# Walking the tokens of the weight-stream matmuls from last to first, with weight tiles at one address distance

## The chip, the core and the metric

The kernel runs on one core of a Trainium2 chip. TensorE (PE) multiplies, VectorE (DVE) and ScalarE (ACT) do elementwise work, GpSimd (POOL) a little of it, and SyncE (SP) issues most of the transfers. SBUF is the working memory of 128 partitions, PSUM the small memory into which TensorE writes. The metric is the time of one execution on the device in microseconds, as the median of several runs; lower is better.

## The reference

Two layers of a hybrid block run over 272 tokens (16 learned ones and 256 of the input) of width 1024. Each layer is a mixer with three branches (retention, a gated recurrence, differential attention) and a feed-forward part with a short convolution. Cut to the products with weights, which the change touches:

```python
def mixer(hn, w_in, w_branch, w_out, ...):
    proj = (hn @ w_in).astype(F32)
    ...
    y_b = jnp.einsum('blnc,ncd->blnd', branches, w_branch.astype(F32))
    gates = jax.nn.sigmoid(mg.reshape(b, l, N_BRANCH, D_MODEL))
    y = jnp.sum(gates * y_b, axis=2)
    return y.astype(hn.dtype) @ w_out

def conv_ffn(hn, w_ffn_in, conv_w, conv_b, w_ffn_out, valid):
    u = jnp.where(valid[None, :, None], hn @ w_ffn_in, 0.0)
    ...
    return (jax.nn.silu(gate) * val) @ w_ffn_out
```

All weights are float32 and are used once per execution.

## The kernel before

Activations lie with features on the partitions and tokens along the row, so a product with a 128 x 128 tile of weights is one matmul whose stationary operand is the weight tile and whose moving operand is a row of up to 272 tokens. The output, 128 output features by the tokens, adds up in a PSUM bank over the 8 (or 22) feature tiles k of the input.

Each float32 operand is split into a high part that TensorE takes exactly in its fast format and a low part that holds the rest. The product is then three passes (lines 915 to 917): high weights by high input, high weights by low input, low weights by high input. This text calls them the stream passes. In layer 0 (and for keys and values in layer 1) a pass has 272 columns, the long form. In layer 1 the others leave out the first 14 tokens (T0) and have 258 columns, the short form. The last product of layer 1 (`fo`, lines 1520 to 1522) is done the other way round, with the weights as moving operand of 512 columns, and isn't part of what the diff edits.

`_Weights.next` (from line 612) brings the weights in chunks of 8 tiles, one DMA of 512 KB each (two halves for the first two). ScalarE writes the high parts to `whi`, VectorE the low parts to `wlo`. Each of these has 4 buffers, the raw chunk 3. Where in its buffer each tile stands is worked out by `_places` (line 131): the start of a tile, modulo 256 bytes (`LINE`), is brought to a wanted value. That value follows the moving operand: rows of 272 words are 1088 bytes, 64 more than a multiple of 256, so it grows by 64 for each k, modulo 256. It has an offset `APART`, one for the long form and one for the short, and 64 more (`BLOCK`) for inputs that lie in other tiles (b0, b1, b2, y, and the gated product). `_runs` (line 156) turns the places into as few instruction patterns as it can.

The moving operands are the normed input (`xh`, `xl`, in pairs of 4 rows of 272 words), the branches' outputs (`b0hi`, `b0lo` and so on), their sum (`yhi`, `ylo`) and the gated product (`ghi`, `glo`). All outputs are the PSUM tile `main`, two banks, one per output tile of a pair.

The order of all instructions is written by a planner (`_Plan`) from modelled costs and due times; each engine then runs its list as it stands. A group of three passes is one operation of the planner. The function `run` inside `products` issues it:

Of the kernel before, what the change touches and what calls it, by code (L numbers as in the profile page):

```python
# [88 lines left out]
def _ktiles(name):  # L89
    return FK if name == "fo" else KD  # L90
# [30 lines left out]


LINE = 256
APART = (0, 200)
BLOCK = 64
ROOM = CHUNK_TILES * P + 2 * LINE // 4
T0 = META - 2
# [3 lines left out]
def _places(depth=DEPTH):  # L131
# [4 lines left out]
    for li in range(depth):  # L136
        for name, j, k, _ in sum(_turns(li), []):
# [3 lines left out]
            short = li == DEPTH - 1 and name not in FULL  # L141
            wants.append(APART[short] + BLOCK * (name[0] == "b" or name in ("wo", "fo")) + 64 * (k % 4))
    out = []
# [497 lines left out]
        return self.cut  # L641


def build(tc, a, depth=DEPTH, probe=None):
    with ExitStack() as ctx:
        plan = _Plan(tc)
        _trace(ctx, tc, plan, a, depth, probe or {})
        plan.issue()
    return plan


def _trace(ctx, tc, plan, a, depth, probe):
# [19 lines left out]
    def new(pool_, shape, dt, tag, bufs, name):  # L672
        serial[0] += 1
        return plan.tile(pool_, shape, dt, tag, bufs, f"{name}_{serial[0]}")
# [217 lines left out]
    def products(xs, name, j, t0=0):  # L892

        if name in BASE or name == "fi":
            norm.next()
        if ahead:
            return ahead.pop()
        tiles = turns.pop(0)
        main = lambda: new(mp, [P, 2, 512], F32, "main", 2, "main")[:, :, t0:T]
        ps = {i: main() for i in sorted({x[1] for x in tiles})}  # L900
        to = {x: ps[x[0]][:, x[1], :] for x in {x[1::2] for x in tiles}}
        if (name, j) == ("fo", 3):

            to[j, 1] = main()[:, 1, :]
        cost = 3 * ((T - t0) / 2400 + 0.003)
        left = dict.fromkeys(to, _ktiles(name))
        for _, i, k, f in tiles:
            hi, lo = (x[:, t0:] for x in xs(k))
            begun = left[i, f] < _ktiles(name)
            left[i, f] -= 1  # L910
            plan.key = clock[0]
            wh, wl = weights.next()

            def run(o=to[i, f], wh=wh, wl=wl, hi=hi, lo=lo, first=not begun, last=left[i, f] == 0):
                nc.tensor.matmul(o, wh, hi, start=first, stop=False)  # L915
                nc.tensor.matmul(o, wh, lo, start=False, stop=False)  # L916
                nc.tensor.matmul(o, wl, hi, start=False, stop=last)  # L917

            plan.main.append(plan.add("pe", run, cost, [to[i, f]], [wh, wl, hi, lo], count=6))
            clock[0] += cost  # L920
        plan.key = clock[0] - 1.0
        if (name, j) == ("fo", 3):
            return [to[j, f] for f in range(2)]
        ahead.extend(ps[i] for i in ps if i != j)
        return ps[j]
# [71 lines left out]
    for li in range(depth):  # L997
# [477 lines left out]
        def block(name):  # L1475
            if name not in st:
                st[name] = slot4(name)
            return st[name]
# [65 lines left out]
        for name, j in ORDER:  # L1544
# [18 lines left out]
            elif name[0] == "*":  # L1563
# [4 lines left out]
                else:  # L1568
                    t = st["rg" if n == "b0" else "hg"]
# [6 lines left out]
            if name in BASE:  # L1576
                lo = 0 if name in FULL else t0
# [17 lines left out]
                elif name in ("dq", "dk"):  # L1595
                    t = block(f"{name}{j // 2}")
# [27 lines left out]
                else:  # L1624
                    t = block(f"{name}{j // 2}")
# [21 lines left out]
            elif name == "wo":  # L1647
                hi, lo = st["yhi"], st["ylo"]
# [40 lines left out]
            else:  # L1689
                hi, lo = st["ghi"], st["glo"]  # L1690
# [35 lines left out]
```

## Time and profile before

| what | value |
|---|---|
| time, median of 3 runs (lowest to highest) | 1301.39 us (1300.91 to 1302.28) |
| span of the profiled execution | 1299.9 us |
| TensorE, matmuls | busy 1290.8 us, 10965 instructions |
| TensorE, loads of weights | busy 1268.7 us, 10965 instructions |
| VectorE | busy 993.4 us |
| ScalarE | busy 855.9 us |
| bytes moved by DMA | 219.01 MB, mean 168 GB/s |
| mean granted TensorE clock | 0.999 |

The span is the time from the first to the last instruction of the one execution that was profiled; the runs' times have a little around it. Busy time of TensorE counts a matmul from its start to the modelled end of its output. Matmuls overlap, so their durations add up to more than the span, and what a pass costs is read from the distance of the starts. In a group's row stand the busy time and the mean duration in ns, and behind the second bar the time that the engine was idle just ahead of these instructions and who ended it. In the rows of a tile stand the smallest, the median and the largest duration.

### The profile page before, as it was taken

To read this page: it belongs to the slowest core of one execution; us is meant where nothing else is said; L and a number is where in the kernel's file an instruction comes from. 1 tells how busy PE (TensorE), PEld (TensorE's weight loads), DVE (VectorE), ACT (ScalarE), POOL (GpSimd) and SP (SyncE) were. 2 spreads that over 40 slices of the span, in tenths; PEclk is the share of its full clock that TensorE was granted. 3 is DMA by queue.
4 is the path that set the end of the run, shared out by engine and by line. 5 is a ranking of instruction groups with operands and counts; after the bars stand their busy time and mean duration, and the time that the engine had idled before them with its cause. 6 is when DMAs were issued, how large, how long until landed. Compare 5 with 4: busy or idle time off the path is not lost.

```text
span 1299.9 us, 27225 instructions
## 1 busy us (share of the span) xinstructions
PE 1290.8 (99%) x10965; PEld 1268.7 (98%) x10965; DVE 993.4 (76%) x1745; ACT 855.9 (66%) x1490; POOL 85.6 (7%) x162
## 2 busy tenths in 40 slices
PE   9999999999999999999999999999999999999998
PEld 8999999999999999999999999999999999999986
DVE  7685888698686789886565868886997868899753
ACT  6765565766777568776456664657667876787743
POOL 5000000000100020000020000000001100200000
PEclk9999999999999999999999999999999999999999
DMA  8555444435544555555555455454444456556653
GB/s 279 195 159 155 167 149 154 146 136 158 162 143 152 180 161 184 187 173 170 178 179 181 161 171 171 146 172 140 149 161 163 146 163 197 173 186 202 201 183 109
DMA packets 60751, 219.01 MB, mean 168 GB/s; under 512 B 6864, under 2 KB 6992, under 8 KB 60624
## 3 DMA queue, kind: packets, MB, share of 16 engines
q1 hardware_dynamic: 60336, 216.74, 51.6%
q8 instruction: 86, 1.41, 0.4%
q10 hardware_dynamic: 288, 0.52, 0.1%
q14 instruction: 41, 0.34, 0.1%
HBM read 216.19 MB, written 1.05 MB: 167 GB/s over the span
## 4 chain that ended last, share of the span: by engine, by line
PE 95%; DVE 3%; DMA 1%; issue 0%; SPq 0%; POOL 0%; ACT 0%; DVEq 0%
PE main L917 28%; PE main L915 28%; PE main L916 27%; PE fo L1520 2%; PE fo L1522 2%; PE fo L1521 2%; PE ds L1383 1%; PE do L593 1%; PE ro L593 1%; PE ho L593 1%; DMA wraw<-in_w 1%; PE vt L593 1%; DVE wlo L593 1%; PE wt L593 0%; PE lev L1106 0%; PE ms L593 0%
## 5 line engine op out<-in xcount | busy, mean ns | idle before, releaser
L915 PE MATMUL main<-xh,whi 128*128 128x272 f32 (+1 forms) x2368 | 687.8, 290 | 0.7 <-ACT whi L593 0.7
L917 PE MATMUL main<-xh,wlo 128*128 128x272 f32 (+1 forms) x2368 | 679.5, 287 | 0.5 <-DVE wlo L593 0.4
L916 PE MATMUL main<-xl,whi 128*128 128x272 f32 (+1 forms) x2368 | 670.4, 283 | 0.0
L593 DVE TENSOR_TENSOR wlo<-wraw,whi 128x1024 fp32r<-128x1024 f32 (+1 forms) x408 | 496.0, 1222 | 198.7 <-ACT whi L593 195.4
L593 ACT ACTIVATE whi<-wraw 128x1024 fp32r<-128x1024 f32 (+1 forms) x408 | 426.5, 1048 | 214.0 <-PE main L916 137.5
L916 PEld LDWEIGHTS main<-xl,whi 128*128 128x128 f32 x2368 | 449.3, 190 | 0.2
L915 PEld LDWEIGHTS main<-xh,whi 128*128 128x128 f32 x2368 | 445.5, 188 | 2.1 <-ACT whi L593 0.9
L917 PEld LDWEIGHTS main<-xh,wlo 128*128 128x128 f32 x2368 | 444.6, 188 | 1.4 <-DVE wlo L593 1.4
L593 DVE SCALAR_TENSOR_TENSOR two_b<-u,small,two_b 128x256 f32<-128x256 f32 (+2 forms) x176 | 78.3, 485 | 0.7 <-ACT two_b L593 0.2
L593 POOL TENSOR_TENSOR y<-h,rstd 128x272 f32<-128x272 f32 x32 | 38.2, 1225 | 311.1 <-ACT rstd L593 311.1
L917 PE MATMUL main<-ghi,wlo 128*128 128x272 f32 x176 | 51.0, 290 | 0.0
L915 PE MATMUL main<-ghi,whi 128*128 128x272 f32 x176 | 50.8, 288 | 0.0
L916 PE MATMUL main<-glo,whi 128*128 128x272 f32 x176 | 50.2, 285 | 0.0
L593 ACT ACTIVATE two_b<-u,small 128x272 f32<-128x272 f32 (+1 forms) x88 | 49.3, 598 | 0.7 <-DVE glo L593 0.5
L593 ACT ACTIVATE u<-main 128x544 f32<-128x544 f32 (+1 forms) x40 | 24.5, 612 | 36.5 <-PE main L917 36.4
L915 PE MATMUL main<-b0hi,whi 128*128 128x272 f32 (+1 forms) x128 | 37.3, 292 | 0.0
L915 PE MATMUL main<-b1hi,whi 128*128 128x272 f32 (+1 forms) x128 | 37.3, 292 | 0.0
L917 PE MATMUL main<-yhi,wlo 128*128 128x272 f32 (+1 forms) x128 | 36.5, 286 | 0.0
L917 PE MATMUL main<-b2hi,wlo 128*128 128x272 f32 (+1 forms) x128 | 36.5, 285 | 0.0
L917 PE MATMUL main<-b0hi,wlo 128*128 128x272 f32 (+1 forms) x128 | 36.5, 285 | 0.0
L917 PE MATMUL main<-b1hi,wlo 128*128 128x272 f32 (+1 forms) x128 | 36.5, 285 | 0.0
L915 PE MATMUL main<-b2hi,whi 128*128 128x272 f32 (+1 forms) x128 | 36.4, 284 | 0.0
(268 smaller groups left out, 1951.7 us busy)
## 6 DMA issues: line engine op xcount, KB each, us to landing
wraw<-in_w SPq DMA_DIRECT2D x402, 512.0 KB, 3.6
h<-in_h SPq DMA_DIRECT2D x4, 272.0 KB, 5.3
dec<-in_dec SPq DMA_DIRECT2D x2, 544.0 KB, 4.5
wraw<-in_w SPq DMA_DIRECT2D x4, 256.0 KB, 5.0
const<-in_const SPq DMA_DIRECT2D x1, 937.0 KB, 6.8
gain<-in_gl SPq DMA_DIRECT2D x1, 512.0 KB, 5.1
out<-y ACTq DMA_DIRECT2D x2, 256.0 KB, 2.7
out<-y SPq DMA_DIRECT2D x2, 256.0 KB, 2.7
```

The costliest lines, as they stand in the source:

```text
L593: self.plan.add(self.name, lambda: f(*args, **kw), cost, outs, ins, args[2] if method == "activation" else None, count)
L915: nc.tensor.matmul(o, wh, hi, start=first, stop=False)
L916: nc.tensor.matmul(o, wh, lo, start=False, stop=False)
L917: nc.tensor.matmul(o, wl, hi, start=False, stop=last)
L1383: nc.tensor.matmul(ss[m][:, at : at + nk], q[half, hd, q0 : q0 + P], k[half, hd, :nk], start=True, stop=True)
L1520: nc.tensor.matmul(o, gh, wh, start=False, stop=False)
L1521: nc.tensor.matmul(o, gl, wh, start=False, stop=False)
L1522: nc.tensor.matmul(o, gh, wl, start=False, stop=end)
```

## The change

```diff
-APART = (0, 200)
+APART = (80, 80)

+def backwards(t):
+
+    return bass.AP(t.tensor, t.offset + t.shape[1] - 1, [list(t.ap[0]), [-1, t.shape[1]]])

             def run(o=to[i, f], wh=wh, wl=wl, hi=hi, lo=lo, first=not begun, last=left[i, f] == 0):
+                o, hi, lo = (backwards(x) for x in (o, hi, lo))
                 nc.tensor.matmul(o, wh, hi, start=first, stop=False)
                 nc.tensor.matmul(o, wh, lo, start=False, stop=False)
                 nc.tensor.matmul(o, wl, hi, start=False, stop=last)
```

`backwards` makes a view of the same words that starts at the last one and steps by -1. In each stream pass the moving operand and the output are walked that way, so token 271 is read first and its column is written first; every token still lands in its own column. The stationary operand, the weight tile, keeps its step of +1 and is contiguous. `APART` sets the weight tiles at another distance from the moving operands, 80 bytes for the long and the short form alike, where it was 0 and 200.

## Prediction

> **What bounds the kernel now.** I read the page's busy shares first, then its chain of waits, then the list of who waited for whom, and then the groups by shape.
>
> ```profile
> span 1299.9 us, 27225 instructions
> PE 1290.8 (99%) x10965; PEld 1268.7 (98%) x10965; DVE 993.4 (76%) x1745; ACT 855.9 (66%) x1490; POOL 85.6 (7%) x162
> PEclk9999999999999999999999999999999999999999
> PE 95%; DVE 3%; DMA 1%; issue 0%; SPq 0%; POOL 0%; ACT 0%; DVEq 0%
> PE warm L593 <- POOL ones_d L593: 1.0, 1, 1.0
> PE main L915 <- ACT whi L593: 0.7, 1, 0.7
> PE main L917 <- DVE wlo L593: 0.4, 2, 0.2
> PE wt L593 <- POOL dt L593: 0.4, 1, 0.4
> PE ro L593 <- DVE am L593: 0.4, 1, 0.4
> PE ro L593 <- DVE wts L593: 0.2, 1, 0.2
> ```
>
> TensorE carries 95% of the chain, at full granted clock, and the last six lines are every wait it had: 3.1 us in all. There is no idle time to win. Only the length of the passes can move the end, and nearly all of them stand on three lines:
>
> ```profile
> L915 PE MATMUL main<-xh,whi 128*128 128x272 f32 x1536 | 450.5, 293 | 0.7 <-ACT whi L593 0.7
> L916 PE MATMUL main<-xl,whi 128*128 128x272 f32 x1536 | 436.7, 284 | 0.0
> L915 PE MATMUL main<-xh,whi 128*128 128x258 f32 x832 | 237.3, 285 | 0.0
> L917 PE MATMUL main<-ghi,wlo 128*128 128x272 f32 x176 | 51.0, 290 | 0.0
> L917 PE MATMUL main<-yhi,wlo 128*128 128x272 f32 x64 | 18.6, 291 | 0.0
> L915 PE MATMUL main<-yhi,whi 128*128 128x258 f32 x64 | 17.9, 280 | 0.0
> ```
>
> Each of the three lines has 1536 long passes on the normed input, 176 on the gated product and 64 each on b0, b1, b2 and y: 1968, so 5904 long ones. Short ones: 832 + 4 x 64 = 1088 a line, 3264 in all. These 9168 are what the diff edits.
>
> A duration of 290 ns is not what a pass costs, because passes overlap. The timeline shows it, with the load of the next weights under each pass:
>
> ```profile
> 539.84 0.28 PE L916 MATMUL main<-xl,whi 128*128 128x272 f32 x1
> 539.85 0.19 PEld L917 LDWEIGHTS main<-xh,wlo 128*128 128x128 f32 x1
> 539.96 0.29 PE L917 MATMUL main<-xh,wlo 128*128 128x272 f32 x1
> 539.97 0.19 PEld L915 LDWEIGHTS main<-xh,whi 128*128 128x128 f32 x1
> 540.09 0.29 PE L915 MATMUL main<-xh,whi 128*128 128x272 f32 x1
> ```
>
> Starts are 0.12 to 0.13 us apart, so some 165 ns of each duration is the tail under the next pass. If that tail is the same for all, a nanosecond off a duration is a nanosecond off the spacing. The means by form above mix in passes that stand behind other work. Two stretches of the feed-forward stage, where nothing but stream passes runs, give the pure values (first the windows, then the tile main in each, as minimum/median/maximum):
>
> ```profile
> 520.00:585.00 65.00, 65.00 (x524) 65.00 (x523) 53.36 (x91) 48.15 (x78) 0.00 (x0) 1.00 0.56 180
> 1105.00:1170.00 65.00, 65.00 (x553) 65.00 (x552) 59.78 (x99) 51.05 (x86) 9.68 (x8) 1.00 0.56 179
> ...
> L917 PE MATMUL main<-xh,wlo x175: 289/291/293, 519.8 to 584.9; 128*128 128x272 f32 x175
> L915 PE MATMUL main<-xh,whi x175: 287/288/290, 519.9 to 585.0; 128*128 128x272 f32 x175
> L916 PE MATMUL main<-xl,whi x174: 282/284/286, 520.0 to 584.7; 128*128 128x272 f32 x174
> ...
> L915 PE MATMUL main<-xh,whi x180: 278/281/288, 1106.3 to 1169.8; 128*128 128x258 f32 x180
> L916 PE MATMUL main<-xl,whi x180: 277/281/288, 1106.4 to 1169.9; 128*128 128x258 f32 x180
> L917 PE MATMUL main<-xh,wlo x179: 278/281/286, 1106.5 to 1169.7; 128*128 128x258 f32 x179
> ```
>
> Spacings are 65/524 = 124.0 ns (long) and 65/553 = 117.5 ns (short). What matters is the three long rows: same shape, same output, no wait, clock 1.00, and yet three ranges that do not touch, 282 to 286 against 289 to 293. They differ in which buffers the pass and the weight load under it read. So up to 11 ns of a pass depends on what is read beside what, and places and directions of reading are what the diff changes.
>
> **The change, part by part.**
>
> *What stays.* The built programs have the same instructions in the same order on all five engines, with the same semaphores and DMAs; operands of the 9168 passes and the places of weight tiles differ. No step is moved past a queue and no wait is added. The splits on ScalarE and VectorE write the same forms to other places: 0 us.
>
> *Step -1 on operand and output.* Every pass reads token 271 first and writes its output column last to first. No row of before has a backward operand. From below: it cannot itself shorten a pass, 0. From above, the nearest pass of as many columns with another manner of reading is the full-precision one:
>
> ```profile
> L1383 PE MATMUL ds<-dk,dq 64*128 64x272 f32 x64 | 10.8, 415 | 0.0
> ```
>
> 415 - 284 = 131 ns more a pass, times 9168 = 1201 us. I take 0: backward neighbours are still neighbours in memory, and pass lengths 272 and 258 are even, so pairs of words stay whole.
>
> The row is 415 against 284 and no row tells more. The Trainium skill's "PSUM — Partial Sum Buffer" (section "Specifications") speaks against the change: PSUM is accessed in lines of 8 bytes, two fp32 values, and a pattern that is not contiguous slows matmuls significantly. Whether -1 counts as contiguous it does not say; by the strict reading the kernel is far slower, which is the third case below.
>
> *Places of the tiles.* In code, the first word of a weight tile stood, modulo 256 bytes, at 0 from the first word that a long pass reads and at 200 - 56 = 144 from that of a short one (it begins 14 words in). Walking backward, both begin at word 271, and the distance is 80 - 1084 = 20 modulo 256 for both. The rate at which the two readings run past each other changes as well, since one direction is turned. What a given distance costs under the new walk no row shows, so I bound it by the extremes of the six rows:
> - Best: every long pass as the shortest long one, 282, against a mean of the medians of (291 + 288 + 284)/3 = 287.7: 5.7 x 5904 = 33 us. Every short one 277 against 281: 4 x 3264 = 13 us. Together 46 us gained.
> - Worst: every long pass 293: 5.3 x 5904 = 31 us; every short one 288: 7 x 3264 = 23 us. Together 54 us lost.
>
> I take the best end. With both readings going one way in place of against each other (if weights are read from the last column, which no row shows) they meet less often, and the L916 row shows that a set of three can hold a pass near 282 for a whole stage. The gain may pass this end, since 282 need not be free of disturbance.
>
> On that floor, the spacing rows are 124.0 and 117.5 ns. The Trainium skill, "TensorE: Matmul & The Clock Gate", section "Back-to-back issue gap", gives columns / 2.4 + 2.5 ns, an estimate of 115.8 and 110.0 here; by it the sum would be (8.2 x 5904 + 7.5 x 3264) = 73 us gained. The same page (Part 2, step on LDWEIGHTS) says that loading the next weights takes no read bandwidth from the running matmul; by that nothing changes. The three separate ranges in one stage speak against it.
>
> *Cover.* A faster TensorE asks for weights sooner. VectorE is busiest in the second window, 59.78 of 65 us; with passes 4 ns of 117.5 shorter the stage takes 62.8 us, 95%. The transfers hold 0.56 of the engines. Neither binds, so I cost lost cover at 0; if the split of a chunk came late once in each mixer stage, that is about 1 us each.
>
> *Sum.* 1299.9 - 46 = 1254 us of span. The three timed runs have a median of 1301.39, 1.5 above the span: **1255 us**.
>
> **The rivals.**
>
> *Slower: the new distance is a bad one.* Between the stream and the load under it the phase is now the same in all 9168 passes; if it is one in which they collide, each pass goes to its long end: 1301.4 + 54 = 1356 us, half of it 1328. It decides as soon as the long median of the feed-forward stage passes 288. For it: ranges to 293 and 288 exist. Against it: if both readings go one way, they meet seldom at any distance, and the short rows, which stood at another distance than the long ones, are no worse for it.
>
> *Slower: the backward step itself breaks the rate,* by the output or by the operand. At the bound 1301 + 1201 = 2502 us; a tenth of it 1421. For it: nothing in the trace, which has no such row. Against it: the even pairs.
>
> *No change.* The spread between the three rows comes from something that neither direction nor place touches, such as the order of high and low halves; then all rows stay and the time is 1301 us. For it: the three rows also differ by line, not only by address. Against it: the short passes, of the same three lines, have one median, 281.
>
> **How the numbers follow.** The forecast gets 0.55, the bad distance 0.28, the broken rate 0.12, no change 0.05. A change under 0.2% (2.6 us) can't be told from none. So faster 0.55, same 0.05, slower 0.40. The forecast's own range is 1225 (somewhat beyond its best end) to 1290 (a quarter of the gain). The whole range reaches from 1225 to 1350, which holds most of the bad distance too; left out are the broken rate (0.12) and some 0.04 at each end.
>
> **What would show it.** In the profile after, the same two windows: spacing of about 118.5 and 113.5 ns, and the three long medians near 282 with no more than a few ns between them. PE's waits stay near 3 us; VectorE's busy time stays at 993 us. If long medians stand at 290 or more with the split between lines as it was, the distance is bad; if all passes of both lengths are longer by one amount, whatever they read beside, the step is to blame; if the last stage's 512-column passes, which aren't edited, change too, I have the cause wrong.

## The result and the profile after

The changed kernel is slower by about half a per cent: a median of 1308.87 us in 4 runs (1308.48 to 1309.32) against 1301.55 us (1300.91 to 1302.28) for the kernel before beside it. The ratio is 1.0056, with a 95% interval of 1.0042 to 1.0070. The span of the profiled execution went from 1299.9 to 1307.2 us.

The page after and the list of TensorE's waits show that the frame of the argument held: the same instructions, TensorE still the bound, no new waits.

```profile
span 1307.2 us, 27225 instructions
PE 1298.7 (99%) x10965; PEld 1277.1 (98%) x10965; DVE 993.9 (76%) x1745; ACT 854.9 (65%) x1490; POOL 83.6 (6%) x162
PE 96%; DVE 2%; DMA 0%; issue 0%; SPq 0%; POOL 0%; ACT 0%; DVEq 0%
PE warm L593 <- POOL ones_d L593: 1.0, 1, 1.0
PE main L923 <- DVE wlo L593: 0.4, 2, 0.2
PE wt L593 <- POOL dt L593: 0.4, 1, 0.4
PE ro L593 <- DVE am L593: 0.3, 1, 0.3
PE ro L593 <- DVE wts L593: 0.3, 1, 0.3
PE main L921 <- ACT whi L593: 0.2, 1, 0.2
```

Lines 921 to 923 are 915 to 917 of before. All waits together are 2.6 us, against 3.1.

Where the 7.3 us arise is seen from the last stream passes of each layer. These are rows of the tile ghi, first of before, then of after; the times behind the durations are the first and the last start.

```profile
L917 PE MATMUL main<-ghi,wlo x176: 282/289/293, 598.0 to 663.6; 128*128 128x272 f32 x176
L1522 PE MATMUL fo<-wlo,ghi x88: 388/392/404, 1233.3 to 1293.6; 128*128 128x512 f32 x88
```

```profile
L923 PE MATMUL main<-ghi,wlo x176: 287/288/293, 598.5 to 664.1; 128*128 128x272 f32 x176
L1528 PE MATMUL fo<-wlo,ghi x88: 388/392/404, 1240.7 to 1300.9; 128*128 128x512 f32 x88
```

Layer 0, all long passes, ends 0.5 us later (664.1 against 663.6). The last product starts and ends some 7.3 us later. So nearly everything was lost in layer 1, where the short passes are; the unedited 512-column passes kept their durations to the nanosecond.

The two pure stretches, taken 3 and 6 us later than in the prediction (first the windows, then the tile main in each), say how:

```profile
523.00:588.00 65.00, 65.00 (x523) 65.00 (x522) 52.37 (x89) 47.31 (x78) 0.00 (x0) 1.00 0.56 176
1111.00:1176.00 65.00, 65.00 (x542) 65.00 (x542) 58.63 (x97) 50.80 (x86) 9.63 (x8) 1.00 0.54 172
...
L922 PE MATMUL main<-xl,whi x175: 288/288/288, 522.8 to 587.9; 128*128 128x272 f32 x175
L923 PE MATMUL main<-xh,wlo x174: 288/290/291, 522.9 to 587.7; 128*128 128x272 f32 x174
L921 PE MATMUL main<-xh,whi x174: 287/288/288, 523.1 to 587.8; 128*128 128x272 f32 x174
...
L921 PE MATMUL main<-xh,whi x179: 279/282/288, 1111.3 to 1175.7; 128*128 128x258 f32 x179
L922 PE MATMUL main<-xl,whi x179: 282/282/288, 1111.4 to 1175.8; 128*128 128x258 f32 x179
L923 PE MATMUL main<-xh,wlo x179: 281/282/288, 1111.6 to 1175.9; 128*128 128x258 f32 x179
```

The durations of the long passes became alike: 282 to 293 before, 287 to 291 now, and the three medians 291, 288, 284 are now 290, 288, 288. They are alike at their old mean, not at their old best: 523 passes in 65 us, where there were 524. The short ones lost their low end. Two of the three minima went from 277 and 278 to 282 and 281, and the stretch holds 542 passes, where it held 553.

Because durations contain the tail under the next pass, I use one more measure below. The **spacing** is the mean distance between the starts of two stream passes that follow each other directly, over the whole trace. It is worked out from the start times in the traces and stands in no view. Distances of 145 ns or more are left out, since the tail of other work stands in them. In the kernel before, that keeps 3144 of 3195 distances behind short passes and 5671 of 5780 behind long ones. For short passes I also give the share of all 3195 that are at most 117 ns, and that are 120 or 121 ns.

| kernel | time, us | long, ns | short, ns | short at most 117 | short 120 or 121 |
|---|---|---|---|---|---|
| before | 1301.55 | 124.6 | 118.1 | 48% | 14% |
| after | 1308.87 | 124.8 | 120.4 | 1% | 92% |
| e1, backward walk at the old places | 1309.39 | 124.8 | 120.3 | 0% | 76% |
| e2, forward walk at the new places | 1309.90 | 124.8 | 120.6 | 21% | 30% |
| e3, forward, many distances | 1309.44 | 125.4 | 119.6 | 28% | 26% |
| e4, backward, many distances | 1311.96 | 125.2 | 120.7 | 2% | 67% |
| e5, as e4, operand alone backward | 1312.33 | 125.2 | 120.7 | 2% | 67% |
| e6, as e4, output alone backward | 1312.60 | 125.4 | 120.2 | 21% | 30% |
| e9, before with half of each load | 1296.78 | 124.3 | 117.7 | 47% | 28% |
| e11, after with half of each load | 1312.93 | 125.8 | 120.3 | 8% | 61% |
| e12, after, all 32 bytes further on | 1309.53 | 124.8 | 120.4 | 1% | 77% |
| e14, before, all 32 bytes further on | 1302.28 | 124.7 | 118.1 | 48% | 14% |
| e13, after without splits and transfers | 1312.48 | 125.4 | 120.6 | 2% | 56% |
| e10, forward at 0 and 148 | 1299.06 | 124.6 | 117.3 | 52% | 16% |

Times are medians of 4 to 11 runs for before, after, e1, e2 and e10, and one run each for the others. As a check on the measure: (120.36 - 118.12) x 3264 = 7.3 us and (124.76 - 124.64) x 5904 = 0.7 us, together 8.0, for a span 7.3 us longer.

Spacing and duration aren't the same measure. The short passes last 282.3 ns on average in the changed kernel and 284.2 in e1, at spacings of 120.4 and 120.3: the tail under the next pass differs by 2 ns between the two kernels.

### The profile page after: what moved, and what is told of

It is laid out like the page before. It is cut to its first block, busy times and chain, and to the rows that moved or that the text cites. A ratio compares the mean times of both kernels' runs of the same rounds, so it can differ in the third digit from the quotient of the medians.

```text
span 1307.2 us, 27225 instructions
## 1 busy us (share of the span) xinstructions
PE 1298.7 (99%) x10965; PEld 1277.1 (98%) x10965; DVE 993.9 (76%) x1745; ACT 854.9 (65%) x1490; POOL 83.6 (6%) x162
## 4 chain that ended last, share of the span: by engine, by line
PE 96%; DVE 2%; DMA 0%; issue 0%; SPq 0%; POOL 0%; ACT 0%; DVEq 0%
PE main L921 28%; PE main L923 28%; PE main L922 28%; PE fo L1526 2%; PE fo L1528 2%; PE fo L1527 2%; PE ds L1389 1%; PE do L593 1%; PE ho L593 1%; PE ro L593 1%; PE vt L593 1%; DMA wraw<-in_w 0%; PE lev L1112 0%; PE wt L593 0%; DVE wlo L593 0%; PE ms L593 0%
## 5 line engine op out<-in xcount | busy, mean ns | idle before, releaser
L922 PE MATMUL main<-b1lo,whi 128*128 128x272 f32 (+1 forms) x128 | 36.5, 285 | 0.0
```

## The experiments

**Walk and place, one at a time (e1, e2).** The changed kernel with the old distances, and the kernel before with the new ones.

```diff
 # e1, against the changed kernel
-APART = (80, 80)
+APART = (0, 200)
 # e2, against the kernel before
-APART = (0, 200)
+APART = (80, 80)
```

> The backward walk with the tiles where before had them (0 and 200). Theory A, the new place is at fault and the walk is harmless: about 1301 us or below, short passes back near a spacing of 118 ns. Theory B, the walk itself lengthens the short passes: still 1308 us or more, short spacing 120 ns or more. Theory C, under the backward walk the distance decides: any value that differs from both, with other minima and maxima in the long and short rows.

> The forward walk with the tiles at 80 for both lengths. Theory A (place at fault): slower than 1301 us by some 7 us, with the loss in the short passes. Theory B (walk at fault): about 1301 us. Theory C (a distance is good or bad only together with a direction): slower or faster by more than 7 us, long and short by different amounts.

Measured: e1 1309.39 us, ratio 1.0059 (1.0046 to 1.0071); e2 1309.90 us, ratio 1.0063 (1.0049 to 1.0077). Either half of the change costs as much as the whole, so the costs don't add and neither theory A nor B alone describes it. The rows of the short stretch differ, though. First e1, then e2:

```profile
1111.00:1176.00 65.00, 65.00 (x543) 65.00 (x542) 58.47 (x98) 50.48 (x85) 9.63 (x8) 1.00 0.56 175
L921 PE MATMUL main<-xh,whi x178: 282/284/286, 1111.7 to 1175.7; 128*128 128x258 f32 x178
L922 PE MATMUL main<-xl,whi x178: 284/284/286, 1111.8 to 1175.8; 128*128 128x258 f32 x178
L923 PE MATMUL main<-xh,wlo x178: 284/284/288, 1111.9 to 1175.9; 128*128 128x258 f32 x178
```

```profile
1111.00:1176.00 65.00, 65.00 (x541) 65.00 (x540) 58.23 (x97) 50.06 (x85) 9.67 (x8) 1.00 0.58 175
L915 PE MATMUL main<-xh,whi x178: 278/282/288, 1111.7 to 1175.9; 128*128 128x258 f32 x178
L916 PE MATMUL main<-xl,whi x177: 277/284/288, 1111.8 to 1175.7; 128*128 128x258 f32 x177
```

Backward, the passes stand close together, nearly all at 284, and none is below 282. Forward at 80 they spread from 277 to 288, as before, only with more of them at the long end.

**A sweep of the distance within one kernel, for both walks (e3, e4).** Each output group gets another distance, so one run gives a curve.

```diff
+SWEPT = [x for x in ORDER if x[0] in BASE]
 ...
-            wants.append(APART[short] + BLOCK * (name[0] == "b" or name in ("wo", "fo")) + 64 * (k % 4))
+            apart = APART[short]
+            if name == "fi":
+                apart = 16 * j if j < 16 else 8 + 40 * (j - 16)
+            elif name in BASE:
+                apart = 20 * (0 if (name, j) == ("hq", 1) else SWEPT.index((name, j))) % 256
+            wants.append(apart + BLOCK * (name[0] == "b" or name in ("wo", "fo")) + 64 * (k % 4))
```

> The forward walk with another distance for each output group: 16 x j bytes for the feed-forward groups j = 0 to 15 (8 + 40 x (j - 16) for the last 6), other multiples of 4 in the mixer. Theory C: spacing of the stream passes changes from group to group by 5 ns or more and is lowest near 0 for the long and near 200 for the short form. Theory B (distance hardly matters): within 2 ns everywhere.

> The same sweep under the backward walk. Theory C: spacing swings by 5 ns or more over the distances; somewhere it falls below 120 ns (long) and 115 ns (short), the lowest of before, and one distance is best for both lengths. Theory B (the walk sets the spacing): near 124 and 120 ns at every distance.

Measured, as spacing by distance. Each value is the mean of 37 to 179 distances within output groups; 54 places were tried for the long form and 39 for the short:

| | lowest | highest | at the distances of before and after |
|---|---|---|---|
| forward, long | 124.2 (0, 12 and 28 bytes) | 127.9 (140) | 124.2 at 0, 124.8 at 80 |
| forward, short | 117.1 (148) | 125.9 (120) | 120.4 at 80 |
| backward, long | 124.3 (4) | 126.6 (220) | 125.1 at 0, 124.8 at 80 |
| backward, short | 120.1 (84) | 123.6 (232) | 120.4 at 80 |

Under the forward walk the distance matters for the short passes, as theory C says (9 ns between the ends), though their best lies at 148 and only the second best, 117.9 ns at 212, is near 200; the long ones gain nothing over the distance 0. The upper ends depend on the cut at 145 ns: with one at 140, the 125.9 would be 123.0. Under the backward walk no distance tried brings the short passes below 120.1 ns or the long ones below 124.3, as theory B says. The distance of 80 is within 0.5 ns of the best for both forms: there was no good distance to be found. The swing at the upper end, up to 3.5 ns, is more than B expected.

**Operand or output (e5, e6).** The backward sweep with only one of the two views reversed. Tokens then land in reversed columns, so these two compute something else.

```diff
 # e5
-                o, hi, lo = (backwards(x) for x in (o, hi, lo))
+                hi, lo = (backwards(x) for x in (hi, lo))
 # e6
-                o, hi, lo = (backwards(x) for x in (o, hi, lo))
+                o = backwards(o)
```

> The backward sweep again, but only the moving operand walks backward; the output is written forward, so tokens land in reversed columns and the result is not the reference's. Theory P, the backward write to PSUM sets the floor of 120 ns of the short passes: short passes go below 120 again, with 115 to 118 common and a mean spacing near the forward sweep's 119.5. Theory S, the direction of the operand's reading against the weight load sets it: short passes stay at 120 to 121 with nearly nothing below 118; long ones at a mean near 125.

> The sweep with only the output written backward and the operand read forward (result not the reference's: tokens reversed). Theory P: short passes gather at 120 and almost none is below 118. Theory S: as the forward sweep, a mean of 119.5 with a wide spread from 115 to 124.

This is theory S. Reversing the operand alone gives the backward sweep back (120.7 and 125.2 ns, and all shares equal); reversing the output alone gives the forward sweep. The rows of one short stretch show it, in the order e4, e5, e6, e3:

```profile
L928 PE MATMUL main<-xl,whi x172: 281/282/290, 1114.0 to 1176.0; 128*128 128x258 f32 x172
```

```profile
L928 PE MATMUL main<-xl,whi x170: 281/282/290, 1114.4 to 1175.6; 128*128 128x258 f32 x170
```

```profile
L928 PE MATMUL main<-xl,whi x169: 277/282/289, 1115.5 to 1176.0; 128*128 128x258 f32 x169
```

```profile
L922 PE MATMUL main<-xl,whi x177: 277/282/289, 1112.4 to 1175.7; 128*128 128x258 f32 x177
```

The first two have 281/282/290, the last two 277/282/289. Writing PSUM backward costs nothing that can be seen. The short spacing of e6 is 0.6 ns above that of e3 over the whole trace, but that is the place: passes that the sweep leaves out (branches and their sum) stand at 200 in e3, as before, and at 80 in e6, as after, with 118.1 and 120.6 ns. The swept short passes, at the same places in both runs, have 120.0 ns in both. Nor do operand and output reversed together (e4) cost anything over the operand alone.

**What the passes wait for: the load of the next weights? (e9, e11)** Weight loads and outputs take 64 of the 128 columns, except in the first and the last pass of each sum, so half of each product is left out.

```diff
-                nc.tensor.matmul(o, wh, hi, start=first, stop=False)
-                nc.tensor.matmul(o, wh, lo, start=False, stop=False)
-                nc.tensor.matmul(o, wl, hi, start=False, stop=last)
+                full = slice(0, 128 if first else 64)
+                nc.tensor.matmul(o[full], wh[:, full], hi, start=first, stop=False)
+                nc.tensor.matmul(o[:64], wh[:, :64], lo, start=False, stop=False)
+                full = slice(0, 128 if last else 64)
+                nc.tensor.matmul(o[full], wl[:, full], hi, start=False, stop=last)
```

> The kernel before with weight loads and outputs of 64 of the 128 columns in all stream passes but the first and the last of each sum, so half of each product is left out. Theory L, what lengthens a pass is the load of the next weights under it: the long spacing falls from 124.6 to below 120 and the short from 118.1 to below 114. Theory O, the weight load has no part in it: 124 and 118 as before.

> The changed kernel with the same halved loads. Theory L: the long spacing falls from 124.7 and the short from 120.4 by 4 ns or more, and the two walks come within 1 ns of each other. Theory O: 124.7 and 120.4 as in the changed kernel.

Theory L falls, as far as the length of the load goes. In the long stretch the load ahead of the second pass of each three is shorter by 55 ns, and the pass is not. First before, then e9:

```profile
L916 PEld LDWEIGHTS main<-xl,whi x175: 189/190/193, 519.9 to 585.0; 128*128 128x128 f32 x175
L916 PE MATMUL main<-xl,whi x174: 282/284/286, 520.0 to 584.7; 128*128 128x272 f32 x174
```

```profile
L917 PEld LDWEIGHTS main<-xl,whi x175: 133/135/137, 520.0 to 584.8; 128*64 128x64 f32 x175
L917 PE MATMUL main<-xl,whi x175: 284/288/290, 520.1 to 584.9; 128*64 128x272 f32 x175
```

Over the whole trace the spacing falls by 0.3 (long) and 0.4 ns (short) forward; backward the long one rises by 1.0 and the short one stays. The gap between the walks stays: 120.3 against 117.7 for the short passes.

**Where a reading begins within 64 bytes (e12, e14).** One small tile ahead of the operands is made larger, which moves operands and weight tiles by 32 bytes together and keeps every distance.

```diff
-    fixed([P, KD], "step")
+    fixed([P, 2 * KD], "step")
```

> The changed kernel with all operands and weight tiles 32 bytes further on, every distance kept. Theory G, a pass's length depends on where its reading begins within a line of 64 bytes (backward both lengths begin at its end): the short passes leave their floor of 120 ns by 1.5 ns or more. Theory R, only the distance and the direction count: 120.4 and 124.8 ns as in the changed kernel, 1308 to 1310 us.

> The kernel before with the same 32 bytes. Theory G: long and short spacings change by 1.5 ns or more from 124.6 and 118.1. Theory R: unchanged, about 1302 us.

This is theory R: spacings within 0.1 ns of the kernels that they were made from. As far as one step of 32 bytes shows, what counts is the place of one against the other, not the place itself.

**Other traffic (e13).** The changed kernel with the first two chunks of weights kept for all stream passes, so that the other chunks are neither transferred nor split (save those of the last product), and the other products take the weights of these two chunks in place of their own. The central lines of the edit:

```diff
 ...
+        if c >= 2 and self.places[c] != self.whole:
+            hi, lo = self.kept[c % 2]
+            at = self.places[c % 2][i]
+            return hi[:, at : at + P], lo[:, at : at + P]
 ...
```

> The changed kernel with the first two chunks of weights used for all stream passes: their transfers and splits on ScalarE and VectorE are left out, save those of the last product. Theory W, writes of the other engines and DMAs into SBUF lengthen the passes: 118 ns or less (long) and 113 or less (short). Theory R: the passes' own reading sets them, 124 to 125 and 120 to 121 ns, and the time stays within 15 us of 1309.

This is theory R again. The long stretch, with the transfers at nothing and VectorE at 29.73 us in place of 52.37, holds 520 passes where it held 523:

```profile
523.00:588.00 65.00, 65.00 (x520) 65.00 (x519) 29.73 (x64) 28.09 (x54) 0.00 (x0) 1.00 0.00 1
```

That it holds fewer is the place again. A kept chunk now meets input rows other than its own, so the tiles stand at 16, 80, 144 and 208 bytes, about a quarter each, and not all at 80. Those at 80 have 124.9 ns (long) and 120.6 (short), against 124.8 and 120.4 in the changed kernel. The long ones at 16, 144 and 208 have 125.5, 126.8 and 124.6, where e4 has 125.7, 126.5 and 124.6 with all the traffic.

**A distance from the forward sweep (e10).**

```diff
-APART = (0, 200)
+APART = (0, 148)
```

> The forward walk with (0, 148): the short distance that had the lowest mean spacing in the forward sweep, 117.1 ns in 44 passes, against 118.1 with 200. If the distance decides under the forward walk, the 3264 short passes come to about 117.1 ns and the time to 1298 us; if those 44 passes were chance, 1301 us or more.

Measured: 1299.06 us in 11 runs, beside 1301.79 us; ratio 0.9980 (0.9971 to 0.9989). The short spacing is 117.3 ns, and (118.12 - 117.32) x 3264 = 2.6 us of the 2.7. It is a mean of unlike steps: the spacing behind the second pass of each three fell from 118.2 to 115.9 ns and behind the third from 118.4 to 117.3, behind the first it rose from 117.8 to 118.8. The second pass, which was 277/281/288 in the short stretch of before, is here:

```profile
1111.00:1176.00 65.00, 65.00 (x558) 65.00 (x557) 60.95 (x103) 53.12 (x90) 9.70 (x8) 1.00 0.58 180
L916 PE MATMUL main<-xl,whi x185: 276/277/287, 1111.0 to 1175.7; 128*128 128x258 f32 x185
```

This is 0.2% faster than the kernel before, and by moving weight tiles alone.

## Why the prediction was wrong

**What bounds the kernel** was right. TensorE has 96% of the chain and 2.6 us of waits; the loss is the length of passes and nothing else. "What stays" was right too: VectorE is busy 993.9 us against 993.4, and the last product is unchanged.

**The step that failed** is the choice between the two ends: "I take the best end", 46 us gained, because both readings would go one way and so "meet less often". Being uniform and being short were taken for one thing. The first came true in the durations: long passes went from 282 to 293 to a range of 287 to 291. The second did not. The backward walk gives the long ones 124.8 ns, where their old mean was 124.6, and the short ones 120.4, 2.2 above theirs, and in e4 no distance betters this by more than 0.5 ns. The spread of the old long rows was no prize. Behind the first, second and third pass of a group the distances were 126.1, 121.8 and 126.3 ns; they are 123.7, 124.2 and 126.4. The sum of the three stays at 374: what the second pass had less, the first had more.

Two readings made the prize look surer. The three long rows were said not to touch, but 287 to 290 and 289 to 293 overlap; only the row of L916 stood apart. And the spacings of 124.0 and 117.5 ns divide 65 us by a count that takes in passes cut by the window's edges; the distances of starts in the same windows give 124.7 and 118.1. (The best end also adds up to 47 us and not 46: 33.7 and 13.1.)

That 1308.87 us lies in the whole range (1225 to 1350) is luck: its upper part was there for passes that all go to their long end, which did not happen.

**The cost of the backward step**, taken as 0, was right for the output (e6). For the operand it was right for the long passes to within 0.2 ns (e1) and wrong for the short ones: reading it backward holds them at 120 ns or more at every place tried (e4, e5). At the old places that is (120.31 - 118.12) x 3264 = 7.1 us, in e1. It is the rival of a broken rate, on its operand side, at 2 ns a short pass, where the bound was 131. And it is a loss only against a good place: at 80, the forward walk has 120.6 ns (e2) and the backward one 120.4.

On the output, the Trainium skill's page "PSUM — Partial Sum Buffer" (section "Specifications") says that a pattern that is not contiguous slows matmuls significantly; in e6 the swept short passes have 120.0 ns, as in e3, so a step of -1 behaves here as contiguous.

**The bad distance**, the largest rival, was to show as long medians above 288; they are 288, 290 and 288, and e4 found no distance more than 0.5 ns better. But its other half holds: 80 is a worse place for the forward walk (e2), so 200 was worth its gain only with the walk that it was found for. This is why the halves don't add: in the changed kernel the old place has lost its value with the walk, and the new one costs nothing more.

**The floor.** The best end was called possibly too cautious, since passes seemed to lose 8 ns each to what is read beside them. No run took that away: not half of the load (e9, e11), not silent transfers and splits (e13), not another start within 64 bytes (e12, e14), not any distance tried. The prediction's estimate of 73 us gained rests on the formula in the Trainium skill's "TensorE: Matmul & The Clock Gate" (section "Back-to-back issue gap"), which the page gives for a matmul in isolation; with a load under each pass the mean spacing came to its 115.8 and 110.0 ns at no place of the sweeps, the lowest being 124.2 and 117.1 (e3). On the load, the same page of the Trainium skill (Part 2, step on LDWEIGHTS) says that it takes no SBUF read bandwidth from the running matmul; with the load 55 ns shorter the spacing moved by 0.3 to 0.4 ns forward and not for the better backward, so as far as the load's length goes the trace agrees. Its place still moves the short spacing, from 118.1 to 120.6 ns in e2 and to 117.3 in e10.

**What stays open.** Why the forward short passes can go to 115 ns and the backward ones gather at 120 is not shown. Whether weights are read from the last column, on which the picture of two readings going one way rested, was not tried; nor were passes with no load under them, or short passes of other lengths under the backward walk.

## What to carry to other kernels

A group whose passes spread from 282 to 293 ns does not offer its minimum to all of them: find out first, in the trace, whether the short ones are paid for by their neighbours, as the sum of 374 ns for three passes showed here. A tuned address distance belongs to the direction of walking for which it was found, so test direction and distance apart; each alone lost what the two lost together. Where a setting can differ from group to group, one kernel that sweeps it gives the whole curve in one run: here it said that no distance tried helps the backward walk, and it found the forward one that gained 2.7 us. Before two runs of such a sweep are compared, make sure that the passes it leaves out stand at the same places in both.

## What had not been expected

- Moving the weight tiles by a fraction of 256 bytes against the operand changes the spacing of short forward passes between 117.1 and 125.9 ns among the groups of e3, and between 117.3 (e10) and 120.6 (e2) over whole kernels.
- The direction in which the operand is read turns a wide pattern (115 to 125 ns) into a single value (92% of short distances at 120 or 121 ns in the changed kernel), at the same or a higher mean.
- Halving the weight load, from about 189 to 135 ns, is worth 0.3 to 0.4 ns a pass with the forward walk and nothing with the backward one.
